# Keys padded with zeros and two heads per product in the scores of a mixer, with some buffers moved

## The chip, the core and the metric

The kernel runs on one core of a Trainium2 chip. The metric is the device time of one whole execution in microseconds (us); smaller is better. A measured time is the median of several runs. A profile is one further execution, recorded by the hardware profiler. The engines are TensorE (PE in the tables; PEld is its weight load), VectorE (DVE), ScalarE (ACT), GpSimd (POOL) and SyncE (SP), which issues most transfers.

## What is computed

The reference is two transformer blocks on 256 tokens of width 1024 in fp32. The change lies in the second block's mixer, which stands twice in the program (stages m0 and m1, two layers):

```python
z = h @ w_in[l]
(na_q, na_k, na_v, gq, gk, gv, gr, gfl, gbl, c_q, c_kv, k_rope, gates) = split_cols_2(z, IN_SPLITS)
qa = rms_norm_2(na_q.reshape(B, S, NA_HEADS, NA_HEAD_DIM), na_q_norm[l])
ka = rms_norm_2(na_k.reshape(B, S, NA_HEADS, NA_HEAD_DIM), na_k_norm[l])
y_na = neighborhood_attention(qa, ka, va, na_rpb[l])
o_gla = gla_bidirectional(gq..., gk..., gv..., g_f..., g_b...)
y_gla = rms_norm_2(o_gla, gla_out_norm[l]).reshape(B, S, GLA_V_W) * silu(gr)
y_mla = mla_attention(c_q, c_kv, k_rope, cq_norm, ckv_norm, w_uq, w_ukv, q_norm, k_norm, cos, sin)
gt = sigmoid(gates.reshape(B, S, N_BRANCH, D))
mixed = gt[:, :, 0] * (y_na @ w_br_na) + gt[:, :, 1] * (y_gla @ w_br_gla) + gt[:, :, 2] * (y_mla @ w_br_mla)
x = x + mixed @ w_out[l]
```

So one mixer has three branches over the same input: neighbourhood attention (NA, 8 heads of 64), gated linear attention (GLA, 4 heads of key width 64 and value width 128, both directions), and latent attention (MLA, 4 heads whose scores add a part of width 128 and a rotary part of width 64).

## The kernel before

A tile scheduler orders the instructions. The Python code says what depends on what and which buffer each value takes; the scheduler plays the program through its own clock and writes one list for each engine. A buffer with the same tag as an older one has the older one's room, so its first writer waits for the older one's last reader. A change of buffers or of an instruction's length therefore changes the lists of all engines in the two mixers; nothing ahead of stage m0 differs.

Weights come as fp32 tiles ("raw"). `prep` splits each into a rounded part (ACT, L149) and a rest (DVE, L153), and `mm3` (L188 to L190) makes three short products of each. Results stand in PSUM banks of [128, 512] from three pools: "pj" (three banks: projections), "pa" (three: scores, transposes, attention values) and "pb" (two: GLA).

In `mixer2`, q and k of NA are transposed (L1346) and copied to "naq" and "nak" with the 64 rows of two heads on top of each other (L1347). `na_scores` makes, for each of two query tiles and each of four pairs of heads, two products on 64 of the 128 array rows (L1357); a pair is two heads that lie in the same half of the rows. DVE adds the bias (L1359). `attention` takes the rest: DVE row maximum (L805), ACT exponential (L807), PE transposes (L815), ACT or DVE copies (L820, L822), PE values (L827), and the close (L833, then the transposes L201).

`gla(f)` is called for two halves of heads, f = 0 and 1. Each is a chain over three engines: gate product (PE, L1452, 32 rows), then ACT L1455, DVE L1456, ACT L1457 (exp), DVE L1458, ACT L1459 (with a load of its function table), five DVE steps (L1460 to L1464), ACT L1470 (again with a table load), DVE L1471, ACT L1474 to L1476, DVE and POOL L1477 to L1479, PE transposes (L1482), an ACT copy (L1483), and only then the state products (PE, L1491, 64 rows), the state steps (DVE, L1499), the inner scores (PE, L1508), the values (PE, L1516 and L1520) and the norm (ACT, L1524). The projection "gr" of GLA's output gate goes from its two pj banks through ACT (L1409) into a buffer "gs" of its own.

`uq_proj` and `ukv_proj` make q, k and v of MLA: squares on ACT (L1561, L1580), scaling on DVE, and `put`, which transposes (PE, L1552 and L1553) and copies to "mq" or "mk" (ACT, L1554). `mla_scores` makes for each head one product on 128 rows (L1600) and one on 64 rows (L1601). The branches' results meet in `mix`, two buffers in the room of "naq" and "nak", gated by `gate` (ACT, L1540).

Of the kernel before, what the change touches and what calls it, by code (L numbers as in the profile page):

```python
# [10 lines left out]
AF = mybir.ActivationFunctionType  # L11
# [55 lines left out]
class Kern:  # L67
# [1223 lines left out]
    def mixer2(self, i, finish):  # L1291
# [31 lines left out]
        nc.gpsimd.memset(hv(rst)[:, :, 0:1], 0.0)  # L1323


        naT = [T([128, 4, 256], "naq"), T([128, 4, 256], "nak")]
        nav = T([128, 2, 512], "nav")
        yna = self.quad()
        na_heads = [[0, 2], [1, 3], [4, 6], [5, 7]]

        def na_proj(j):
            if j == 2:
                self.proj_nat(hT, 8, W, (i,), [(1024, 512)], lambda t, p: nc.scalar.activation(nav[:, t, :], p, AF.Copy))
                return

            def ev_na(t, p):
                sq = g2()
                nc.scalar.activation(sq, p, AF.Square)
                ss = self.small([128, 8], "nss")
                nc.vector.tensor_reduce(ss, hv(sq), axis=AX.X, op=OP.add)  # L1340
                r = self.rstd(ss, 8, 1.0 / 64, "na")
                x = g2()
                nc.vector.tensor_tensor(hv(x), hv(p), r.unsqueeze(2).to_broadcast([128, 8, 64]), op=OP.mult)
                q = self.pa()
                for k in range(4):
                    nc.tensor.transpose(q[:, k * 128:k * 128 + 128], x[:, k * 128:k * 128 + 128], ident)  # L1346
                nc.scalar.activation(naT[j][:, :, t * 128:t * 128 + 128], hv(q, 128), AF.Copy, scale=nag[:, j:j + 1])  # L1347
            self.proj_nat(hT, 8, W, (i,), [(j * 512, 512)], ev_na, first=j == 0)

        def na_scores(t, hs):  # L1350
            bias = T([128, 512], "sE", bufs=2).rearrange("p (h n) -> p h n", h=2)
            s = na_heads.index(hs)
            nc.sync.dma_start(bias, A["na_bias"][i][t][:, 2 * s:2 * s + 2, :])
            q = self.pa()
            b = slice(hs[0] % 2 * 64, hs[0] % 2 * 64 + 64)
            for j, h in enumerate(hs):
                nc.tensor.matmul(q[:, j * 256:j * 256 + 256], naT[0][b, h // 2, t * 128:t * 128 + 128], naT[1][b, h // 2, :],  # L1357
                                 start=True, stop=True)
# [43 lines left out]
            nc.vector.tensor_copy(gk[:, f, :], p[:, :256])  # L1402

        gv = T([128, 2, 512], "gv")
        gs = T([128, 2, 512], "gs")

        def ev_gr(t, p):
            y = gs[:, t, :]
# [36 lines left out]
        def gla(f):  # L1445
# [56 lines left out]
            for b in range(2):  # L1502
                bs = slice(b * 64, b * 64 + 64)
                h = f * 2 + b
                q = self.pb()
                for j in range(4):
                    js = slice(j * 128, j * 128 + 128)
                    nc.tensor.matmul(q[:, js], d_[bs, js], c_[bs, js], start=True, stop=True)  # L1508
                Ah = At[:, b * 256:b * 256 + 256].rearrange("p (t n) -> p t n", t=2)
                qv = q.rearrange("p (d t n) -> p d t n", d=2, t=2)  # L1510
                for d, m in ((0, mF), (1, mB)):
                    nc.vector.copy_predicated(Ah, col(m).to_broadcast([128, 2, 128]), qv[:, d])
                o = self.pb()
                for t in range(2):
                    os = slice(t * 128, t * 128 + 128)
                    nc.tensor.matmul(o[:, os], Ah[:, t, :], gv[:, t, h * 128:h * 128 + 128], start=True, stop=False)  # L1516
                    todo = [(n, d) for n in (2 * t, 2 * t + 1) for d in range(2) if (n > 0 if d == 0 else n < 3)]
                    for n, d in todo:
                        s = n - 1 if d == 0 else 2 - n
                        nc.tensor.matmul(o[n % 2 * 64:n % 2 * 64 + 64, os], c_[bs, d * 256 + n * 64:d * 256 + n * 64 + 64],  # L1520
                                         st[bs, d, s, :], start=False, stop=(n, 1 - d) not in todo or d == 1)
                for t in range(2):
                    jk = T([128, 128], "jk2", BF16)
                    nc.scalar.activation(jk[:, :128], o[:, t * 128:t * 128 + 128], AF.Square, accum_out=gss[:, t, h:h + 1])  # L1524
                    r = self.rstd(gss[:, t, h:h + 1], 1, 4.0 / 128, "g", 4 * EPS)
                    y = gs[:, t, h * 128:h * 128 + 128]
                    nc.vector.scalar_tensor_tensor(y, o[:, t * 128:t * 128 + 128], r, y, op0=OP.mult, op1=OP.mult)
            if f == 1:
                for t in range(2):
                    self.to_T(gs[:, t, :], t, ygl, bank=self.pb)  # L1530


        th = {}
# [7 lines left out]
            self.proj_nat(hT, 8, W, (i,), [(3680 + b * 1024 + n * 512, 512)], ev_g)  # L1541


        mq, mk = T([128, 2, 3, 256], "mq"), T([128, 2, 3, 256], "mk")
        mv = T([128, 2, 512], "mv")
        mss = T([128, 2, 2, 4], "mss")

        def put(t, half, nope, rp, dst):

            q = self.pa()  # L1550
            for k in range(2):
                nc.tensor.transpose(q[:, k * 128:k * 128 + 128], nope(k), ident)  # L1552
            nc.tensor.transpose(q[:, 256:384], rp, ident)  # L1553
            nc.scalar.activation(dst[:, half, :, t * 128:t * 128 + 128], hv(q[:, :384], 128), AF.Copy)  # L1554

        def uq_proj(half):
            def ev_uq(t, p):
                jk = T([128, 192], "jk3", BF16)
                for j in range(2):
                    h = half * 2 + j  # L1560
                    nc.scalar.activation(jk[:, :192], p[:, j * 192:j * 192 + 192], AF.Square, accum_out=mss[:, t, 0, h:h + 1])  # L1561
                r = self.rstd(mss[:, t, 0, half * 2:half * 2 + 2], 2, 1.0 / 192, "uq")
                x = g2()
# [6 lines left out]
                put(t, half, lambda k: x[:, k * 192:k * 192 + 128], o.rearrange("p h n -> p (h n)"), mq)  # L1570
            self.proj_nat([cq], 2, "mla_w_uq_2", (i,), [(half * 384, 384)], ev_uq)

        def ukv_proj(half):
            def ev_kv(t, p):
                pv = hv(p, 256)
                nc.vector.tensor_copy(hv(mv[:, t, half * 256:half * 256 + 256], 128), pv[:, :, 128:256])
# [12 lines left out]
                put(t, half, lambda k: x[:, k * 128:k * 128 + 128], x[:, 256:384], mk)  # L1589
# [4 lines left out]
        def mla_scores(t, hs):  # L1594
            q = self.pa()
            ts = slice(t * 128, t * 128 + 128)
            for j, h in enumerate(hs):
                out = q[:, j * 256:j * 256 + 256]
                b = slice(h % 2 * 64, h % 2 * 64 + 64)
                nc.tensor.matmul(out, mq[:, h // 2, h % 2, ts], mk[:, h // 2, h % 2, :], start=True, stop=False)  # L1600
                nc.tensor.matmul(out, mq[b, h // 2, 2, ts], mk[b, h // 2, 2, :], start=False, stop=True)  # L1601
            return hv(q, 256), T([128, 512], "sE", bufs=2).rearrange("p (h n) -> p h n", h=2)

        def mla_att():
            self.attention(T, [(t, hs) for t in range(2) for hs in ([0, 2], [1, 3])], mla_scores,
                           lambda b, h: mv[:, b, h * 128:h * 128 + 128], 128, ymla, self.pa, self.pa, 1, 0)


        mix = [T([128, 1024], n) for n in ("naq", "nak")]
        xq = [None, None]  # L1610
        done = {}

# [134 lines left out]
def constants(inputs):  # L1747
# [27 lines left out]
    rpb = np.asarray(inputs["na_rpb_2"])[:, [0, 2, 1, 3, 4, 6, 5, 7]]  # L1775
# [30 lines left out]
```

## Time and profile before

| | us |
|---|---|
| median of 3 runs | 2415.28 (2411.58 to 2416.04) |
| time of the profiled execution | 2414.7 |
| span of its trace | 2412.9 |
| PE busy | 2384.6 (99% of the span) |
| DVE, ACT, POOL busy | 1470.6 (61%), 1209.5 (50%), 178.1 (7%) |
| mean granted PE clock | 0.997 |

In the trace m0 lies at about 1290 to 1530 us and m1 at about 1950 to 2190 us. The page's part 1 gives the busy time of each engine; part 4 follows back the chain of work that ended last and gives each engine's share of it. In the rows further below, a timeline row has its start, its duration, the engine, the line, the operation, what it writes and reads, its shape (rows x columns of the stationary operand, then partitions x elements of the moving one) and a count. Matmuls overlap, so a product's cost is the step from its start to the next one's start, not its duration.

### The profile page before, as it was taken

The numbers are of one execution on the slowest core, as the hardware profiler recorded it, in microseconds if no ns is written. First come the engines' busy times: TensorE is split into PE (matmuls) and PEld (weight loads), VectorE is DVE, ScalarE is ACT, GpSimd is POOL, SyncE is SP. The second block draws the span as 40 slices with busy tenths as digits, with TensorE's granted clock in tenths as the row PEclk, the third lists the DMA queues.
The fourth block names the chain that finished last, engine by engine and source line by source line (L and its number), as shares of the span: only waits on it lengthen the run. The fifth ranks groups of instructions, "written<-read, shape, count | busy, mean of one in ns | idle before, by whom it ended". The sixth has DMA issues, their size and how long they took to land.

```text
span 2412.9 us, 31370 instructions
## 1 busy us (share of the span) xinstructions
PE 2384.6 (99%) x11520; PEld 1960.4 (81%) x11520; DVE 1470.6 (61%) x2082; ACT 1209.5 (50%) x1868; POOL 178.1 (7%) x185
## 2 busy tenths in 40 slices
PE   8999999999999999999999999999999999999999
PEld 6888988888888778888888777888888887778887
DVE  6556786555655765556556775655565567756554
ACT  5445554444544545445445563454454455635443
POOL 0000330000000400000001120100000011201000
PEclk9999999999999999999999999999999999999999
DMA  7666535665665426656666533566566574435654
GB/s 246 190 189 182 148 123 177 200 190 170 207 212 168 130 69 203 190 167 209 187 188 189 159 119 111 174 206 190 170 205 191 175 205 143 118 120 168 201 189 134
DMA packets 301258, 417.13 MB, mean 173 GB/s; under 512 B 29168, under 2 KB 227248, under 8 KB 301104
## 3 DMA queue, kind: packets, MB, share of 16 engines
q1 hardware_dynamic: 300960, 414.66, 55.7%
q8 instruction: 90, 1.47, 0.2%
q14 instruction: 64, 0.52, 0.1%
q10 hardware_dynamic: 144, 0.48, 0.0%
HBM read 414.01 MB, written 1.05 MB: 172 GB/s over the span
## 4 chain that ended last, share of the span: by engine, by line
PE 96%; DVE 1%; POOL 1%; DMA 1%; ACT 1%; issue 1%; SPq 0%; POOLq 0%; DVEq 0%; ACTq 0%
PE pb L189 13%; PE pb L188 13%; PE pb L190 13%; PE pj L188 13%; PE pj L190 13%; PE pj L189 13%; PE pa L201 3%; PE pa L188 2%; PE pa L189 2%; PE pa L190 2%; PE pj L59 2%; PE pa L59 1%; PE pa L827 1%; PE pa L1357 1%; PE pa L815 0%
## 5 line engine op out<-in xcount | busy, mean ns | idle before, releaser
L153 DVE TENSOR_TENSOR wl<-raw,wh 128x1024 fp32r<-128x1024 f32 x711 | 879.0, 1242 | 548.1 <-ACT wh L149 544.0
L149 ACT ACTIVATE wh<-raw 128x1024 fp32r<-128x1024 f32 x717 | 753.1, 1055 | 572.2 <-PE pb L190 321.3
L188 PE MATMUL pb<-wh,qh 128*128 128x512 f32 x1408 | 551.3, 392 | 0.8 <-ACT wh L149 0.8
L189 PE MATMUL pb<-wl,qh 128*128 128x512 f32 x1408 | 550.3, 391 | 0.5 <-DVE wl L153 0.5
L190 PE MATMUL pb<-wh,ql 128*128 128x512 f32 x1408 | 549.8, 390 | 0.0
L188 PEld LDWEIGHTS pb<-wh,qh 128*128 128x128 f32 x1408 | 264.6, 188 | 56.5 <-ACT wh L149 1.2
L189 PEld LDWEIGHTS pb<-wl,qh 128*128 128x128 f32 x1408 | 264.6, 188 | 56.0 <-DVE wl L153 1.0
L190 PEld LDWEIGHTS pb<-wh,ql 128*128 128x128 f32 x1408 | 264.7, 188 | 55.5
L188 PE MATMUL pj<-wh,qh 128*128 128x512 f32 (+1 forms) x674 | 267.7, 400 | 0.7 <-ACT qh L204 0.7
L189 PE MATMUL pj<-wl,qh 128*128 128x512 f32 (+1 forms) x674 | 264.9, 393 | 1.2 <-DVE wl L153 1.2
L190 PE MATMUL pj<-wh,ql 128*128 128x512 f32 (+1 forms) x674 | 264.0, 395 | 0.0
L190 PE MATMUL pj<-wh,gl 128*128 128x512 f32 x432 | 173.8, 402 | 0.0
L189 PE MATMUL pj<-wl,gh 128*128 128x512 f32 x432 | 168.5, 390 | 0.0
L188 PE MATMUL pj<-wh,gh 128*128 128x512 f32 x432 | 168.3, 391 | 0.0
L446 ACT ACTIVATE sg<-pb,nr 128x256 f32<-128x256 f32 x176 | 83.4, 474 | 151.7 <-PE pb L190 151.6
L188 PEld LDWEIGHTS pj<-wh,qh 128*128 128x128 f32 x674 | 126.9, 189 | 29.5 <-issue 4.3
L190 PEld LDWEIGHTS pj<-wh,ql 128*128 128x128 f32 x674 | 126.9, 188 | 29.3 <-issue 2.7
L189 PEld LDWEIGHTS pj<-wl,qh 128*128 128x128 f32 x674 | 127.2, 189 | 26.8 <-DVE wl L153 2.0
L448 DVE SCALAR_TENSOR_TENSOR g<-pb,nr,sg 128x256 f32<-128x256 f32 x176 | 84.6, 481 | 93.7 <-ACT sg L446 93.7
L204 ACT ACTIVATE gh<-pa 128x256 fp32r<-128x256 f32 x176 | 67.2, 382 | 129.9 <-PE pa L201 129.8
L273 POOL TENSOR_TENSOR nr<-nm,mhalf 128x1 f32<-128x1 f32 x24 | 14.2, 593 | 1444.7 <-DVE nm L271 1444.7
L205 DVE TENSOR_TENSOR gl<-pa,gh 128x256 fp32r<-128x256 f32 x176 | 74.3, 422 | 71.3 <-ACT gh L204 64.0
(538 smaller groups left out, 2993.0 us busy)
## 6 DMA issues: line engine op xcount, KB each, us to landing
raw<-in_ffn_w SPq DMA_DIRECT2D x352, 256.0 KB, 3.1
raw<-in_w_in SPq DMA_DIRECT2D x104, 512.0 KB, 4.0
raw<-in_ffn_w_gate SPq DMA_DIRECT2D x176, 256.0 KB, 2.9
raw<-in_ffn_w_up SPq DMA_DIRECT2D x176, 256.0 KB, 3.1
raw<-in_ffn_w_down SPq DMA_DIRECT2D x88, 512.0 KB, 3.6
raw<-in_ffn_w SPq DMA_DIRECT2D x88, 512.0 KB, 3.5
raw<-in_hy_w_in SPq DMA_DIRECT2D x44, 512.0 KB, 3.7
raw<-in_hy_w_out SPq DMA_DIRECT2D x16, 512.0 KB, 3.3
```

The costliest lines, as they stand in the source:

```text
L59: self.last = fn(*a, **k)
L149: nc.scalar.activation(h[:, :n], r[:, :n], AF.Copy)
L153: eng.tensor_tensor(l[:, :n], r[:, :n], h[:, :n].bitcast(F32), op=OP.subtract)
L188: mm(out, a[0], b[0], start=start, stop=False)
L189: mm(out, a[0], b[1], start=False, stop=False)
L190: return mm(out, a[1], b[0], start=False, stop=stop)
L201: pe = nc.tensor.transpose(p[:, k * 128:(k + 1) * 128], src[:, k * 128:(k + 1) * 128], self.ident)
L204: act = nc.scalar.activation(hv, pv, AF.Copy)
L205: dve = nc.vector.tensor_tensor(lv, pv, hv.bitcast(F32), op=OP.subtract)
L446: nc.scalar.activation(sg, q[t][:, :256], AF.Silu, scale=rs[t])
L448: nc.vector.scalar_tensor_tensor(g, q[t][:, 256:], rs[t], sg, op0=OP.mult, op1=OP.mult)
L827: at["V", k] = nc.tensor.matmul(acc[t][:, h * dv:h * dv + dv], PT[:, j * 2 + b, :], vals(b, h), start=b == 0, stop=b == 1)
```

## The change

The keys get zeros where the other head of a pair has its rows. "nak" grows to [128, 4, 2, 256]: for each pair the first copy holds the upper head's keys and zeros in rows 64 to 127, the second the reverse. POOL writes the zeros; the one ACT copy of the keys becomes two of 64 rows. One product on all 128 rows with 512 columns then gives the scores of both heads, and a pair is now two neighbouring heads. MLA's rotary keys are padded likewise in a new buffer "mr" [128, 2, 2, 256], so that two 64-row products become one of 128 rows and 512 columns, and the one ACT copy of a key tile becomes three (L1568 and twice L1571). "mk" shrinks by a third.

Room for the larger "nak" is found by moving: "gs" loses its own buffer and takes that of "naq" (free after the last NA score), "mr" takes that of "nav" (free after the last NA value), and `mix` lies wholly in that of "nak". A constant's order of heads follows the new pairs.

```diff
-        naT = [T([128, 4, 256], "naq"), T([128, 4, 256], "nak")]
+        naq, nak = T([128, 4, 256], "naq"), T([128, 4, 2, 256], "nak")
+        nc.gpsimd.memset(nak[64:128, :, 0, :], 0.0)
+        nc.gpsimd.memset(nak[0:64, :, 1, :], 0.0)
...
-                nc.scalar.activation(naT[j][:, :, t * 128:t * 128 + 128], hv(q, 128), AF.Copy, scale=nag[:, j:j + 1])
+                for b in range(2):
+                    bs = slice(b * 64, b * 64 + 64)
+                    nc.scalar.activation(nak[bs, :, b, ts], hv(q[bs], 128), AF.Copy, scale=nag[bs, 1:2])
...
-            for j, h in enumerate(hs):
-                nc.tensor.matmul(q[:, j * 256:j * 256 + 256], naT[0][b, h // 2, t * 128:t * 128 + 128], naT[1][b, h // 2, :],
-                                 start=True, stop=True)
+            nc.tensor.matmul(hv(q, 256), naq[:, hs[0] // 2, t * 128:t * 128 + 128], nak[:, hs[0] // 2], start=True, stop=True)
...
-        gs = T([128, 2, 512], "gs")
+        gs = []
...
+            if not gs:
+                gs.append(T([128, 2, 512], "naq"))
...
-            nc.scalar.activation(dst[:, half, :, t * 128:t * 128 + 128], hv(q[:, :384], 128), AF.Copy)
+            nc.scalar.activation(mk[:, half, :, ts], hv(q[:, :256], 128), AF.Copy)
+            for b in range(2):
+                bs = slice(b * 64, b * 64 + 64)
+                nc.scalar.activation(mr[0][bs, half, b, ts], q[bs, 256:384], AF.Copy)
...
+                mr.append(T([128, 2, 2, 256], "nav"))
+                nc.gpsimd.memset(mr[0][64:128, :, 0, :], 0.0)
+                nc.gpsimd.memset(mr[0][0:64, :, 1, :], 0.0)
...
-            for j, h in enumerate(hs):
-                out = q[:, j * 256:j * 256 + 256]
-                b = slice(h % 2 * 64, h % 2 * 64 + 64)
-                nc.tensor.matmul(out, mq[:, h // 2, h % 2, ts], mk[:, h // 2, h % 2, :], start=True, stop=False)
-                nc.tensor.matmul(out, mq[b, h // 2, 2, ts], mk[b, h // 2, 2, :], start=False, stop=True)
+            nc.tensor.matmul(hv(q, 256), mq[:, p, 2, ts], mr[0][:, p], start=True, stop=False)
+            for j in range(2):
+                nc.tensor.matmul(q[:, j * 256:j * 256 + 256], mq[:, p, j, ts], mk[:, p, j, :], start=False, stop=j == 1)
...
-        mix = [T([128, 1024], n) for n in ("naq", "nak")]
+        mix2 = T([128, 2, 1024], "nak")
+        mix = [mix2[:, 0, :], mix2[:, 1, :]]
```

Lines of the changed code are given with their own numbers; what was L1357, L1409, L1452, L1482, L1491, L1508, L1516 and L1520 is L1364, L1417, L1460, L1490, L1499, L1516, L1524 and L1528 there, the chain L1455 to L1479 is L1463 to L1487, and `put` is L1563 to L1571.

The lists move in m0 and m1. Names in them: "gs" or "naq" the output gate of GLA, "pj_", "pa_", "pb_" the PSUM banks, "wh" and "wl" a weight tile's two parts, "w" the GLA chain's buffers, "th" the branch gates.

ACT around the eviction of gr in m0, before:

```order
L1459 ACT_TABLE_LOAD
L1459 ACTIVATE w_2649_12223<-w_2648_12222 128x512
L807 ACT_TABLE_LOAD
L807 ACTIVATE sE_11675,rs_11674<-sE_11675,snm_11681 128x256 x2
L1409 ACTIVATE gs_11224<-pj_12084 128x512
L1470 ACTIVATE dec_12238<-w_2648_12222 128x4 x2
L1475 ACTIVATE w_2648_12222<-w_2648_12222 128x512
```

The same place now, from the copy that ends half 0's transposes on:

```order
L1491 ACTIVATE w_2649_12225<-pb_12251 128x512
L1603 ACTIVATE jk_2638_12183,mss_11234<-pj_12162 128x128 x2
L807 ACTIVATE sE_11694,rs_11672<-sE_11694,snm_11699 128x256 x2
L807 ACTIVATE sE_11714,rs_11672<-sE_11714,snm_11719 128x256 x2
L149 ACTIVATE wh_12498<-raw_12496 128x768
L1603 ACTIVATE jk_2643_12204,mss_11234<-pj_12163 128x128 x2
L1417 ACTIVATE naq_12152<-pj_12078 128x512
L1417 ACTIVATE naq_12152<-pj_12079 128x512
```

The first eviction of gr stood in the middle of half 0's chain; both now stand behind that chain's last step.

PE in half 0 of GLA in m0, before, about the first state products:

```order
L188 MATMUL pj_12474<-wh_12168,qh_11080 128x512
L189 MATMUL pj_12474<-wl_12169,qh_11080 128x512
L1491 MATMUL pb_12256<-gv_11223,w_2649_12223 128x256
L1491 MATMUL pb_12260<-gv_11223,w_2649_12223 128x256
L190 MATMUL pj_12474<-wh_12168,ql_11081 128x512
L188 MATMUL pj_12474<-wh_12478,qh_11080 128x512
L189 MATMUL pj_12474<-wl_12479,qh_11080 128x512
L190 MATMUL pj_12474<-wh_12478,ql_11081 128x512
```

The same stretch now, from its last weight product to the first value products:

```order
L190 MATMUL pj_12163<-wh_12100,ql_11227 128x512
L1499 MATMUL pb_12278<-gv_11225,w_2649_12225 128x256
L827 MATMUL pa_11689<-nav_11217,sPT_11708 128x64 x4
L1516 MATMUL pb_12283<-w_2648_12224,w_2649_12225 128x128 x4
L815 MATMUL pa_11723<-const_81,sE_11714 128x128 x2
L1364 MATMUL pa_11736<-nak_11214,naq_11213 128x512
L815 MATMUL pa_11723<-const_81,sE_11714 128x128 x2
L1524 MATMUL pb_12290<-gv_11225,w_2649_12225 128x128
L1528 MATMUL pb_12290<-st_12257,w_2648_12224 64x128 x3
```

The long projection that lay between the steps of GLA (the gate of branch 0, "pj_12474") has moved behind half 0.

ACT in half 1 of GLA in m1, before:

```order
L1455 ACTIVATE w_3929_17988<-pb_17990,gb_16852 128x256 x2
L1457 ACTIVATE w_3929_17988<-w_3929_17988 128x512
L1554 ACTIVATE mk_16878<-pa_18314 128x3x128
L1554 ACTIVATE mq_16877<-pa_18256 128x3x128
L149 ACTIVATE wh_18425<-raw_18423 128x1024
L1459 ACT_TABLE_LOAD
L1459 ACTIVATE w_3930_17989<-w_3929_17988 128x512
```

The same place now:

```order
L1568 ACTIVATE mk_16881<-pa_17866 128x2x128
L1571 ACTIVATE nav_17808<-pa_17866 64x128 x2
L1463 ACTIVATE w_3929_17992<-pb_17994,gb_16854 128x256 x2
L1548 ACTIVATE th_18201<-pj_18126 128x512
L149 ACTIVATE wh_18269<-raw_18267 128x1024
L1465 ACTIVATE w_3929_17992<-w_3929_17992 128x512
L1578 ACTIVATE jk_3980_18223,mss_16883<-pj_18203 128x192
L149 ACTIVATE wh_18331<-raw_18329 128x1024
L1578 ACTIVATE jk_3980_18223,mss_16883<-pj_18203 128x192
L1467 ACT_TABLE_LOAD
L1467 ACTIVATE w_3930_17993<-w_3929_17992 128x512
```

Half 1's chain now shares the queue with the squares of uq (L1578) and with a branch gate (L1548), which came before or after it.

## Rows read from the trace of the kernel before

**Rows 1.** The page: busy time of PE and its weight load; chain by engine.
```profile
PE 2384.6 (99%) x11520; PEld 1960.4 (81%) x11520; DVE 1470.6 (61%) x2082; ACT 1209.5 (50%) x1868; POOL 178.1 (7%) x185
PE 96%; DVE 1%; POOL 1%; DMA 1%; ACT 1%; issue 1%; SPq 0%; POOLq 0%; DVEq 0%; ACTq 0%
```

**Rows 2.** Waits of PE: waiting line, releaser: us in total, times, longest.
```profile
PE pa L201 <- DVE sE L833: 3.4, 4, 0.9
```

**Rows 3.** Groups by line and shape: busy us, mean ns | idle before.
```profile
L1357 PE MATMUL pa<-nak,naq 64*128 64x256 f32 x64 | 19.5, 422 | 0.0
L1601 PE MATMUL pa<-mk,mq 64*128 64x256 f32 x32 | 11.1, 428 | 0.0
L1600 PE MATMUL pa<-mk,mq 128*128 128x256 f32 x32 | 10.6, 412 | 0.0
```

**Rows 4.** Timeline of PE around one group of NA scores in m0.
```profile
1315.40 0.28 PE L190 MATMUL pj<-qh,wl 128*96 128x256 f32 x1
1315.61 1.13 PE L1357 MATMUL pa<-nak,naq 64*128 64x256 f32 x4
1316.66 0.39 PE L188 MATMUL pj<-qh,wh 128*128 128x256 f32 x1
1316.89 0.28 PE L189 MATMUL pj<-ql,wh 128*128 128x256 f32 x1
1317.01 0.28 PE L190 MATMUL pj<-qh,wl 128*128 128x256 f32 x1
```

**Rows 5.** Timeline of PE in the MLA scores of m0.
```profile
1438.00 0.59 PE L1600 MATMUL pa<-mk,mq 128*128 128x256 f32 x2
1438.52 0.70 PE L1601 MATMUL pa<-mk,mq 64*128 64x256 f32 x2
1439.15 0.70 PE L1600 MATMUL pa<-mk,mq 128*128 128x256 f32 x2
```

**Rows 6.** Timeline of PE in the first block: an fp32 product with 512 columns.
```profile
311.71 1.02 PE L649 MATMUL pa<-hin,bct 128*128 128x512 f32 x2
312.57 0.60 PE L704 MATMUL pb<-v,kw 128*128 128x257 f32 x2
```

**Rows 7.** Timeline of PE: products on different halves of the rows.
```profile
1396.28 0.48 PE L1357 MATMUL pa<-nak,naq 64*128 64x256 f32 x1
1396.29 0.48 PE L1491 MATMUL pb<-gv,w 64*128 64x256 f32 x1
```

**Rows 8.** Windows: us, then PE, PEld, DVE, ACT, POOL busy (count), clock, DMA share, GB/s.
```profile
1379.41:1406.79 27.38, 27.38 (x143) 21.08 (x142) 22.68 (x50) 13.64 (x38) 5.24 (x7) 1.00 0.52 162
1420.25:1448.15 27.90, 27.90 (x125) 20.95 (x124) 21.26 (x34) 19.58 (x36) 5.15 (x7) 1.00 0.44 132
1411.30:1414.70 3.40, 3.05 (x16) 2.83 (x17) 2.21 (x7) 1.73 (x5) 1.06 (x3) 0.50 0.32 120
```

**Rows 9.** Timeline of ACT in half 1 of GLA in m0; in brackets idle before, releaser.
```profile
1421.29 0.85 ACT L1455 ACTIVATE w<-pb,gb 128x256 f32<-128x256 f32 x2
1423.19 0.63 ACT L1457 ACTIVATE w<-w 128x512 f32<-128x512 f32 x1 [1.05 <-DVE w L1456]
1423.73 0.47 ACT L1554 ACTIVATE mk<-pa 128x384 f32<-128x384 f32 x1
...
1425.40 1.06 ACT L149 ACTIVATE wh<-raw 128x1024 fp32r<-128x1024 f32 x1 [0.82 <-PE pj L190]
1426.48 1.28 ACT L1459 ACT_TABLE_LOAD   x1
...
1432.90 1.28 ACT L1470 ACT_TABLE_LOAD   x1 [0.83 <-DVE w L1463]
...
1442.83 0.60 ACT L1483 ACTIVATE w<-pb 128x512 f32<-128x512 f32 x1 [2.58 <-PE pb L1482]
```

**Rows 10.** Groups of ACT from 1404 to 1450 us by shape: the short kinds.
```profile
L1561 ACT ACTIVATE jk<-pj 128x192 bf16<-128x192 f32 x5 | 1.6, 330 | 1.3 <-PE pj L190 1.3
L1470 ACT ACTIVATE dec<-w 128x4 f32<-128x4 f32 x2 | 0.4, 200 | 0.0
```

More of the change, by code (lines that the diff above doesn't have):

```diff
@@ L1323, in mixer2 @@
         nc.gpsimd.memset(hv(rst)[:, :, 0:1], 0.0)
-        naT = [T([128, 4, 256], "naq"), T([128, 4, 256], "nak")]
+        naq, nak = T([128, 4, 256], "naq"), T([128, 4, 2, 256], "nak")
+        nc.gpsimd.memset(nak[64:128, :, 0, :], 0.0)
+        nc.gpsimd.memset(nak[0:64, :, 1, :], 0.0)
         nav = T([128, 2, 512], "nav")
         yna = self.quad()
-        na_heads = [[0, 2], [1, 3], [4, 6], [5, 7]]
+        na_heads = [[0, 1], [2, 3], [4, 5], [6, 7]]
         def na_proj(j):
@@ L1346, in ev_na @@
                     nc.tensor.transpose(q[:, k * 128:k * 128 + 128], x[:, k * 128:k * 128 + 128], ident)
-                nc.scalar.activation(naT[j][:, :, t * 128:t * 128 + 128], hv(q, 128), AF.Copy, scale=nag[:, j:j + 1])
+                ts = slice(t * 128, t * 128 + 128)
+                if j == 0:
+                    nc.scalar.activation(naq[:, :, ts], hv(q, 128), AF.Copy, scale=nag[:, 0:1])
+                    return
+                for b in range(2):
+                    bs = slice(b * 64, b * 64 + 64)
+                    nc.scalar.activation(nak[bs, :, b, ts], hv(q[bs], 128), AF.Copy, scale=nag[bs, 1:2])
             self.proj_nat(hT, 8, W, (i,), [(j * 512, 512)], ev_na, first=j == 0)
@@ L1354, in na_scores @@
             q = self.pa()
-            b = slice(hs[0] % 2 * 64, hs[0] % 2 * 64 + 64)
-            for j, h in enumerate(hs):
-                nc.tensor.matmul(q[:, j * 256:j * 256 + 256], naT[0][b, h // 2, t * 128:t * 128 + 128], naT[1][b, h // 2, :],
-                                 start=True, stop=True)
+            nc.tensor.matmul(hv(q, 256), naq[:, hs[0] // 2, t * 128:t * 128 + 128], nak[:, hs[0] // 2], start=True, stop=True)
             nc.vector.tensor_tensor(bias, hv(q, 256), bias, op=OP.add)
@@ L1404, in mixer2 @@
         gv = T([128, 2, 512], "gv")
-        gs = T([128, 2, 512], "gs")
+        gs = []
         def ev_gr(t, p):
-            y = gs[:, t, :]
+            if not gs:
+                gs.append(T([128, 2, 512], "naq"))
+            y = gs[0][:, t, :]
             nc.scalar.activation(y, p, AF.Tanh, scale=0.5)
@@ L1525, in gla @@
                     r = self.rstd(gss[:, t, h:h + 1], 1, 4.0 / 128, "g", 4 * EPS)
-                    y = gs[:, t, h * 128:h * 128 + 128]
+                    y = gs[0][:, t, h * 128:h * 128 + 128]
                     nc.vector.scalar_tensor_tensor(y, o[:, t * 128:t * 128 + 128], r, y, op0=OP.mult, op1=OP.mult)
@@ L1529, in gla @@
                 for t in range(2):
-                    self.to_T(gs[:, t, :], t, ygl, bank=self.pb)
+                    self.to_T(gs[0][:, t, :], t, ygl, bank=self.pb)
         th = {}
@@ L1541, in gate, with put @@
             self.proj_nat(hT, 8, W, (i,), [(3680 + b * 1024 + n * 512, 512)], ev_g)
-        mq, mk = T([128, 2, 3, 256], "mq"), T([128, 2, 3, 256], "mk")
+        mq, mk = T([128, 2, 3, 256], "mq"), T([128, 2, 2, 256], "mk")
+        mr = []
         mv = T([128, 2, 512], "mv")
         mss = T([128, 2, 2, 4], "mss")
-        def put(t, half, nope, rp, dst):
+        def put(t, half, nope, rp, keys):
             q = self.pa()
+            ts = slice(t * 128, t * 128 + 128)
             for k in range(2):
@@ L1553, in put @@
             nc.tensor.transpose(q[:, 256:384], rp, ident)
-            nc.scalar.activation(dst[:, half, :, t * 128:t * 128 + 128], hv(q[:, :384], 128), AF.Copy)
+            if not keys:
+                nc.scalar.activation(mq[:, half, :, ts], hv(q[:, :384], 128), AF.Copy)
+                return
+            nc.scalar.activation(mk[:, half, :, ts], hv(q[:, :256], 128), AF.Copy)
+            for b in range(2):
+                bs = slice(b * 64, b * 64 + 64)
+                nc.scalar.activation(mr[0][bs, half, b, ts], q[bs, 256:384], AF.Copy)
         def uq_proj(half):
@@ L1569, in ev_uq @@
                 rope(o, xr, t, 2)
-                put(t, half, lambda k: x[:, k * 192:k * 192 + 128], o.rearrange("p h n -> p (h n)"), mq)
+                put(t, half, lambda k: x[:, k * 192:k * 192 + 128], o.rearrange("p h n -> p (h n)"), False)
             self.proj_nat([cq], 2, "mla_w_uq_2", (i,), [(half * 384, 384)], ev_uq)
         def ukv_proj(half):
+            if not mr:
+                mr.append(T([128, 2, 2, 256], "nav"))
+                nc.gpsimd.memset(mr[0][64:128, :, 0, :], 0.0)
+                nc.gpsimd.memset(mr[0][0:64, :, 1, :], 0.0)
             def ev_kv(t, p):
@@ L1588, in ev_kv @@
                     nc.vector.tensor_scalar(x[:, 256 + j * 64:320 + j * 64], kro[:, t, :], r[:, j:j + 1], None, op0=OP.mult)
-                put(t, half, lambda k: x[:, k * 128:k * 128 + 128], x[:, 256:384], mk)
+                put(t, half, lambda k: x[:, k * 128:k * 128 + 128], x[:, 256:384], True)
             self.proj_nat([(cq[0][:, :, 2:4, :], cq[1][:, :, 2:4, :])], 2, "mla_w_ukv_2", (i,), [(half * 512, 512)], ev_kv)
@@ L1596, in mla_scores @@
             ts = slice(t * 128, t * 128 + 128)
-            for j, h in enumerate(hs):
-                out = q[:, j * 256:j * 256 + 256]
-                b = slice(h % 2 * 64, h % 2 * 64 + 64)
-                nc.tensor.matmul(out, mq[:, h // 2, h % 2, ts], mk[:, h // 2, h % 2, :], start=True, stop=False)
-                nc.tensor.matmul(out, mq[b, h // 2, 2, ts], mk[b, h // 2, 2, :], start=False, stop=True)
+            p = hs[0] // 2
+            nc.tensor.matmul(hv(q, 256), mq[:, p, 2, ts], mr[0][:, p], start=True, stop=False)
+            for j in range(2):
+                nc.tensor.matmul(q[:, j * 256:j * 256 + 256], mq[:, p, j, ts], mk[:, p, j, :], start=False, stop=j == 1)
             return hv(q, 256), T([128, 512], "sE", bufs=2).rearrange("p (h n) -> p h n", h=2)
         def mla_att():
-            self.attention(T, [(t, hs) for t in range(2) for hs in ([0, 2], [1, 3])], mla_scores,
+            self.attention(T, [(t, hs) for t in range(2) for hs in ([0, 1], [2, 3])], mla_scores,
                            lambda b, h: mv[:, b, h * 128:h * 128 + 128], 128, ymla, self.pa, self.pa, 1, 0)
-        mix = [T([128, 1024], n) for n in ("naq", "nak")]
+        mix2 = T([128, 2, 1024], "nak")
+        mix = [mix2[:, 0, :], mix2[:, 1, :]]
         xq = [None, None]
@@ L1774, in constants @@
     dc = np.clip(cc[None, :] - cc[:, None] + 15, 0, 30)
-    rpb = np.asarray(inputs["na_rpb_2"])[:, [0, 2, 1, 3, 4, 6, 5, 7]]
+    rpb = np.asarray(inputs["na_rpb_2"])
     c0 = np.clip(cc[:, None] - 8, 0, 48)
```

## Prediction

> **What bounds the kernel now.** I read the page first, then the waits of PE, its timeline in the score products, and last the windows and ACT's timeline in GLA. The page says that PE is busy for 99% of the span and makes 96% of the chain that ended last [rows 1]. So time goes only if PE's own steps get shorter, and comes only if PE waits. In the mixers it hardly waits: the one line there is 3.4 us in four waits at the close of attention, none longer than 0.9 us [rows 2]. DVE and ACT are busy for 61% and 50%, but in places they are nearer to the limit than that: while half 0 of GLA runs, DVE is busy 22.68 of 27.38 us, and in half 1 ACT is busy 19.58 of 27.90 us, while PE is busy all through both [rows 8]. There PE doesn't wait because long projections stand between the steps of GLA.
>
> **What the change takes away.** A product on 64 rows beside products on 128 rows costs more than its columns. In [rows 4] the short products step by 0.12 us (1316.89 to 1317.01). The step into the group is 0.21 (1315.40 to 1315.61), so 0.09 more; the first product behind it takes 0.23, so 0.11 more; and the four passes of the group take 1.05 (1315.61 to 1316.66). The new form is one product of 512 columns on all rows. [rows 6] has two such products' passes in a row: 0.86 us for two passes (311.71 to 312.57), which is what one NA product of two passes will take. So 1.05 - 0.86 = 0.19 inside, 0.20 at the edges: 0.39 a group. There are 16 groups (two layers, two query tiles, four pairs; 64 passes in [rows 3]): 6.2 us.
>
> In MLA each change between 128 and 64 rows costs: two passes take 0.63 us (1438.52 to 1439.15) [rows 5], where half of a 512-column pass would make 0.43. A pair of heads has eight passes, four times 0.63 = 2.5 us. New: two passes of 512 columns, 0.86, and four of 256, 0.86, together 1.72. That is 0.78 a pair, and 8 pairs (32 passes each of L1600 and L1601 [rows 3]) make 6.2 us. The columns streamed don't change; only the switches go. **Saving: 12.4 us.** The rows are close to what will run, so I bound it by 11 and 14.
>
> **What it adds on PE.** In one place of each layer the scheduler had put an NA score on one half of the rows beside a state product on the other half. They start 0.01 us apart and each lasts 0.48 [rows 7], so one of the two is free. A product on 128 rows can't share. That is some 0.25 us in each layer: **+0.5**. The Trainium skill speaks against this change here: its page "TensorE: Matmul & The Clock Gate" (table under "Why this matters for your kernels") says that products with few rows, placed in different row groups, run concurrently, and padding gives that up. The trace agrees in this one place, but in the groups of [rows 4] all four passes lie on the same half, and none overlaps. By that rule the padding gives up these 0.5 us and no more, since neither kernel puts a pair's two heads on different halves; by rows without any overlap it would give up nothing.
>
> **What it adds elsewhere.** ACT gets one more copy for each key tile of NA and two more for each of MLA, all of half the rows or fewer columns than the copy they replace, 0.47 us [rows 9]; POOL gets four fills in each layer (POOL is busy 5 us of 28 [rows 8]). Neither engine is a bound over the whole mixer, so I cost these at nothing except where they stand in front of GLA's chain (below). The fill of "mr" waits on POOL for the last NA value product and holds what is queued behind it there, the powers of the norms (L218); the transfers on SP keep their number.
>
> **What it moves.** This decides. "gs" now takes the room of "naq", so ACT can't evict gr until the last NA score has read "naq". The products of gr fill two of the three "pj" banks, and these stay occupied. Only one bank is left for projections, and the scheduler runs the rest of GLA's half 0 and of NA with little between. In the lists the long gate projection stands behind half 0 (see the change), and meets the projections of uq and ukv together with half 1, whose products are short.
>
> *Half 0, between its transposes and its first values.* Before, this stretch had 27.38 us of PE work [rows 8]. Now I count there 24 transposes and value passes of NA, three NA groups, the twelve state passes, eight inner-score passes and 6 weight products, at the steps above and at those of the same kinds in the trace some 11.0 us in m0. DVE has 33 instructions there instead of 50. At the stretch's mean (22.68/50 = 0.454 us [rows 8]) they take 15.0 us. So PE can wait up to 4.0 us; at the least nothing, since DVE may come in ahead. In m1 24 more weight products stand in it, and the wait is nearer to nothing at its end but the same at its start. I take 1.6 in each layer, below the middle: **+3.2** (0 to 8).
>
> *Half 1, between its gate product and its first state product.* Before: 27.90 us, PE busy for all of it [rows 8]. In that time the chain passed through ACT and DVE with pauses: 1.05 us before L1457, 0.83 before the second table load, 2.58 before the last copy [rows 9]. Now PE has only 12.6 us of work there in m0 and 13.0 in m1, since the gates' long weight products now stand ahead of the gate product or behind the state products. ACT's list for it in m0: four weight roundings (1.06 each, one of them shorter) 4.0, two table loads 2.57, nine steps on 512 columns at 0.60 to 0.63 5.5, and some 22 short ones between 0.20 and 0.47 [rows 9, 10], 6.3; together 18.4. Back to back they overlap by 0.10 (1423.19 + 0.63 is 1423.82, the next starts at 1423.73 [rows 9]), 3.0 for 30, so 15.4. To that come the chain's pauses, in which ACT has nothing ready: 1.05 + 0.83 and, of the last, the transposes alone, some 0.8: 2.7. So 18.1 - 12.6 = 5.5 us that PE waits, say **+5.4**. In m1 the load is 15.7, and six copies of MLA's keys (1.9) stand right in front of the chain's first step: 15.7 + 2.7 + 1.9 - 13.0 = 7.3, say **+7.2**. The bounds: 15.4 - 12.6 = 2.8 in each layer if the chain's pauses are filled; 27.9 - 13.0 = 15 in each if the chain is no quicker than before.
>
> *Behind it.* The first transposes of uq and the state steps come out in a queue that has no slack left. The nearest row is the close of attention, 0.9 us a wait [rows 2]; I take two in each layer: **+3.6** (0 to 8). One of the two closes in each layer that PE waits for now lies in this stretch and falls away: **-1.7**, half of 3.4 [rows 2].
>
> *Clock.* After such a wait before the trace has stretches in which the granted clock is 0.50, the lower of its two levels: 3.40 us from 1411.30 on [rows 8], where the close of attention in m0 waits. Not every such wait has one. A stretch of 3.4 us costs at most 1.7. I take one more in each layer: **+3.4** (0 to 8).
>
> **Sum.** 3.2 + 5.4 + 7.2 + 3.6 - 1.7 + 3.4 + 0.5 - 12.4 = +9.2. The profiled execution took 2414.7, close to the median of 2415.28, so 2423.9: **2424**. The saving is a sure 12 us of shorter steps; the waits are an uncertain 20.
>
> **The rivals.**
> (1) *The waits are hidden.* DVE and ACT take the chain's steps early enough, because both are idle for a third of the mixer, and only the saving is left: 2414.7 - 12.4 + 0.5 = 2403. For it: 99% busy now, with the same chains. Against it: [rows 8] shows DVE at 83% and ACT at 70% in these very stretches, with twice the PE work beside them.
> (2) *Saving and waits cancel.* With the floors, 2 x 2.8 in half 1, nothing in half 0, 3.6 behind it and one fall of the clock in each layer, 5.6 + 3.6 + 3.4 = 12.6 against 12.4 + 1.7 - 0.5 = 13.6: 2413.7, about the time before. It decides if ACT's pauses fill up with the roundings of weights that the scheduler has put there.
> (3) *Half 1 is no quicker than before.* The chain took 21.5 us from L1455 to L1483 (1421.29 to 1442.83 [rows 9]) because ACT and DVE do other work between its steps; if it takes as long again, PE waits up to 15 us in each layer, and the clock falls twice in each: 2414.7 - 12.4 + 30 + 7 - 1.7 + 0.5 = 2438, with the waits of half 0 about 2440.
> (4) *The fill of "mr" holds POOL* until NA's last value, and the powers (L218) of c and of the outer norms behind it come late: two waits of the close's size in each layer, 3.6, on top of the forecast: 2427. It lies within the forecast's range.
>
> **How the numbers follow.** The forecast, with (4), has 0.58, and (3) 0.06; both are slower but for the forecast's lower edge. (2) has 0.22, (1) 0.14. About 0.2% (4.8 us) is what a measurement of this kernel can tell from no change: 2410.4 to 2420.1. The forecast's own range is 2416 to 2438: its lower end is 5.4 + 7.2 less by half and no fall of the clock, its upper end the halves' upper thirds. Its lower edge gives 0.02 to "same". So faster 0.14, same 0.24, slower 0.62. For 8 in 10 the range leaves out most of (1) and the outer part of (3): 2409 to 2439.
>
> **What would show it.** In the profile after: PE's busy time down by about 12 us with its instructions' count nearly the same; L1364 in steps of 0.43 with no 0.2 at its edges; L1621 and L1623 likewise; in PE's waits new rows at L1490, L1499 and L1563 for ACT or DVE, 15 to 25 us together; stretches at clock 0.50 behind them; L1417 behind the last L1364. The prediction is wrong if those waits are under 8 us together (then (1) or (2)), if the group steps stay near 1.05 us (then the padding doesn't take the switch away), or if the time comes from a stage outside m0 and m1, whose lists are unchanged.

## The result, and the profile after

| | median of the runs, us | ratio to before (95% interval) |
|---|---|---|
| before | 2415.66 (2411.58 to 2416.16, 4 runs) | |
| changed | 2430.77 (2425.07 to 2431.28, 4 runs) | 1.0062 (1.0050 to 1.0074) |

The change makes the kernel slower by 15 us (0.6%). The forecast was 2424. The profiled execution of the changed kernel took 2431.15 us; its page begins:

```profile
span 2429.4 us, 31311 instructions
PE 2383.5 (98%) x11472; PEld 1959.6 (81%) x11472; DVE 1468.8 (60%) x2082; ACT 1217.1 (50%) x1888; POOL 183.1 (8%) x193
PE 94%; ACT 2%; DVE 2%; DMA 1%; POOL 1%; issue 1%; SPq 0%; POOLq 0%; DVEq 0%; ACTq 0%
```

Against [rows 1]: 48 passes fewer on PE, 16 for MLA and 32 for NA, and yet PE is busy for nearly the same time (its shorter steps are nearly met by others that got longer, see the table below), and ACT and DVE have 2% of the chain each instead of 1%. The waits of PE in the mixers, us in total, times, longest (the lines not shown lie outside the mixers or are under 0.8 us):

```profile
PE pa L1563 <- DVE g L1583: 5.0, 1, 5.0
PE pb L1490 <- POOL w L1485: 4.2, 2, 2.5
...
PE pa L1563 <- DVE g L1609: 2.3, 2, 1.3
...
PE pa L201 <- DVE sE L833: 1.8, 2, 0.9
PE pb L1499 <- ACT w L1491: 1.5, 2, 0.8
...
PE pj L188 <- ACT th L1548: 1.1, 1, 1.1
PE pa L815 <- ACT sE L807: 1.0, 2, 0.6
...
PE pb L1516 <- DVE st L1507: 0.9, 1, 0.9
...
PE pb L1499 <- DVE st L1505: 0.9, 1, 0.9
```

Where [rows 2] had one line of 3.4 us, there is now a list. It names the places in GLA's two halves and the transposes of uq and ukv behind them.

The saving is there too. By line and shape (busy us, mean ns), where [rows 3] had 41.2 us in its three lines:

```profile
L1364 PE MATMUL pa<-nak,naq 128*128 128x512 f32 x32 | 17.5, 629 | 0.0
L1623 PE MATMUL pa<-mk,mq 128*128 128x256 f32 x32 | 8.5, 382 | 0.0
L1621 PE MATMUL pa<-nav,mq 128*128 128x512 f32 x16 | 8.2, 593 | 0.0
```

These make 34.2 us, 7.0 less. What the edges of a group cost stands in the steps of its neighbours, so these lines show only a part.

The third thing is the clock. Windows of the changed kernel, columns as in [rows 8]:

```profile
1419.60:1433.40 13.80, 13.03 (x38) 8.77 (x38) 8.20 (x29) 4.81 (x20) 4.59 (x9) 0.51 0.36 108
1436.60:1440.20 3.60, 2.98 (x8) 2.35 (x9) 3.23 (x14) 0.00 (x0) 1.37 (x3) 0.53 0.50 146
2088.60:2092.20 3.60, 3.10 (x9) 2.38 (x10) 3.60 (x11) 0.78 (x3) 2.83 (x5) 0.53 0.02 7
2098.80:2105.80 7.00, 6.06 (x16) 4.53 (x16) 4.26 (x13) 1.59 (x5) 3.24 (x6) 0.51 0.38 111
```

With another fall at 1361.6 these are 30.7 us at the lower level in the two mixers. Before had 10.2: the stretch of 3.4 us in [rows 8], and one in m1:

```profile
2022.29:2029.12 6.83, 6.71 (x19) 4.97 (x20) 5.11 (x11) 4.09 (x6) 1.07 (x1) 0.50 0.44 122
```

They begin at waits or soon behind them: the one at 1419.6 after waits of 1.14 us (until 1415.5) and 1.70 us (until 1418.9).

**Where the 15 us come from.** I took every step of PE in the two mixers (start of one pass to the start of the next) and set it against the median step of the same kind (same shapes of it and its neighbours) in the traces of this case. What is over splits into idle time, steps in the stretches at the lower clock, and the rest. From the first transposes of a mixer to the first step that is the same in both kernels again:

| both mixers, us | usual steps | idle | extra at lower clock | rest | sum |
|---|---|---|---|---|---|
| before | 413.5 | 3.5 | 4.6 | 2.2 | 423.8 |
| changed | 402.0 | 20.0 | 11.7 | 5.0 | 438.8 |
| difference | -11.5 | +16.5 | +7.1 | +2.8 | +15.0 |

How these sums split depends on which steps count as one kind: other choices of neighbours give the usual steps a difference of 9 to 15 us, and the lower clock one of up to 9. The idle time and the sums don't depend on it.

Everything outside the mixers takes 1989.1 us before and 1990.6 after (1.2 of that difference lies before m0, where nothing changed).

**The longest wait, read step by step.** Timeline of the changed kernel in half 1 of m1, rows of several engines:

```profile
2083.67 0.40 PE L190 MATMUL pj<-wh,ql 128*128 128x512 f32 x1
2083.85 0.33 ACT L1578 ACTIVATE jk<-pj 128x192 bf16<-128x192 f32 x1
...
2084.28 1.28 ACT L1467 ACT_TABLE_LOAD   x1
...
2085.58 0.63 ACT L1467 ACTIVATE w<-w 128x512 f32<-128x512 f32 x1
...
2086.11 0.31 ACT L1578 ACTIVATE jk<-pj 128x192 bf16<-128x192 f32 x1
...
2087.25 0.70 POOL L218 TENSOR_TENSOR uqr<-uqm,mhalf 128x2 f32<-128x2 f32 x1 [0.73 <-DVE uqm L216]
...
2087.81 0.23 DVE L1605 TENSOR_SCALAR mss<-mss,krs 128x2 f32<-128x2 f32 x1 [0.63 <-ACT jk L1603]
2087.94 0.69 DVE L1469 TENSOR_TENSOR w<-w,w 128x512 f32<-128x512 f32 x1
2088.54 0.74 DVE L1583 SCALAR_TENSOR_TENSOR g<-pj,uqr,qrow 128x192 f32<-128x192 f32 x2
...
2089.10 0.71 PE L1563 MATMUL pa<-const,g 128*128 128x128 f32 x2 [5.04 <-DVE g L1583]
2089.47 0.78 PE L188 MATMUL pj<-wh,qh 128*128 128x512 f32 x1
...
2090.04 0.63 PE L189 MATMUL pj<-wl,qh 128*128 128x512 f32 x1
```

uq has two token tiles here. On ACT the squares of one (2083.85) come out ahead of GLA's table load and its logarithm (L1467), those of the other (2086.11) behind them. The norms go on to POOL, and the first scaling on DVE (L1583) stands behind a step of ukv that waits for ACT (L1605) and a step of GLA's chain (L1469). Meanwhile PE has the next transposes at the head of its queue. The clock is at its lower level from 2088.7 on, still within this wait: the weight products behind it take 0.63 us instead of 0.40.

**The releaser behind it.** The row that tells why the lists look like this is not a wait of PE. ACT's first eviction of gr in m0, before:

```profile
1370.50 0.60 ACT L1409 ACTIVATE gs<-pj 128x512 f32<-128x512 f32 x1 [0.53 <-PE pj L190]
```

ACT of the changed kernel in m0:

```profile
1378.66 0.60 ACT L1491 ACTIVATE w<-pb 128x512 f32<-128x512 f32 x1 [0.74 <-PE pb L1490]
...
1391.69 0.60 ACT L1417 ACTIVATE naq<-pj 128x512 f32<-128x512 f32 x1 [1.72 <-PE pa L1364]
```

The eviction of gr waits for the last NA score (L1364, 1390.63), since it writes into the room of "naq". The last product of gr, counted in the program's order (the 48th weight product behind the transposes of c), ended at 1376.8, so from there on two of the three pj banks lay full for 15 us (13.5 in m1).

### The profile page after: what moved, and what is told of

Same layout as the page of the kernel before. It is cut to its first block, busy times and chain, and to the rows that moved or that the text cites. A ratio compares the mean times of both kernels' runs of the same rounds, so it can differ in the third digit from the quotient of the medians.

```text
span 2429.4 us, 31311 instructions
## 1 busy us (share of the span) xinstructions
PE 2383.5 (98%) x11472; PEld 1959.6 (81%) x11472; DVE 1468.8 (60%) x2082; ACT 1217.1 (50%) x1888; POOL 183.1 (8%) x193
## 4 chain that ended last, share of the span: by engine, by line
PE 94%; ACT 2%; DVE 2%; DMA 1%; POOL 1%; issue 1%; SPq 0%; POOLq 0%; DVEq 0%; ACTq 0%
PE pb L189 13%; PE pb L188 13%; PE pb L190 13%; PE pj L189 12%; PE pj L188 12%; PE pj L190 12%; PE pa L201 3%; PE pa L188 2%; PE pa L189 2%; PE pa L190 2%; PE pj L59 2%; PE pa L59 1%; PE pa L827 1%; PE pa L1364 1%; PE pa L815 0%
```

## The experiments

Theory R says that this hold of the banks takes the long projections out of the stretches of GLA, and makes the waits. Theory P says that the padding itself does it, by its copies on ACT and its fills on POOL.

**gs in a buffer of its own.** "mk" can take the room of "naq" instead, because MLA's keys are written after the last NA score anyway.

```diff
-                gs.append(T([128, 2, 512], "naq"))
+                gs.append(T([128, 2, 512], "gs"))
...
-        mq, mk = T([128, 2, 3, 256], "mq"), T([128, 2, 2, 256], "mk")
+        mq, mk = T([128, 2, 3, 256], "mq"), []
...
             if not mr:
+                mk.append(T([128, 2, 2, 256], "naq"))
                 mr.append(T([128, 2, 2, 256], "nav"))
```

> The changed kernel, but gs keeps a buffer of its own and mk takes the room of naq (free by the time MLA's keys are written). Theory R (gs in the room of naq holds two pj banks until the last NA score, and so takes the projections away from between GLA's steps): the waits of PE in both mixers fall from 20 us to about the 3.4 of before, the stretches at the lower clock go with them, and the saving of the shorter score products is left: 2415.7 - 12 = about 2404 (2400 to 2408). Theory P (the padding's own extra copies on ACT and fills on POOL make the waits): still about 2430. In the lists between a half's gate product and its first state product stand 78 and 98 weight products again (before 77 and 92, changed kernel 54 and 47 to 54).

2399.42 us (2397.76 to 2400.05), ratio to before 0.9939 (0.9928 to 0.9951): 16 us faster than before, 31 faster than the changed kernel, with the same padding, copies and fills. Its page:

```profile
span 2396.1 us, 31306 instructions
...
PE 2367.7 (99%) x11472; PEld 1950.4 (81%) x11472; DVE 1469.2 (61%) x2082; ACT 1215.3 (51%) x1888; POOL 181.2 (8%) x193
```

Waits of PE in the mixers, the two largest:

```profile
PE pa L201 <- DVE sE L833: 1.8, 2, 0.9
...
PE pj L188 <- DVE g L1583: 1.0, 2, 0.5
```

Timeline of ACT, its eviction of gr in m0:

```profile
1368.64 0.60 ACT L1417 ACTIVATE gs<-pj 128x512 f32<-128x512 f32 x1 [0.53 <-PE pj L190]
...
1374.56 0.60 ACT L1417 ACTIVATE gs<-pj 128x512 f32<-128x512 f32 x1
```

gr is evicted in the middle of half 0's chain again, the waits are gone, and no stretch of the mixers is at the lower clock. Theory P falls: its costs are all still there. It is faster than expected because the 4.6 us that the lower clock cost before are gone too (I had left that out). The saving itself is as expected: the usual steps shrank by 13.5 us and the rest grew by 1.6, 12 together.

**gs in the room of naq, and nothing else.** The kernel before with the reuse alone.

```diff
-        gs = T([128, 2, 512], "gs")
+        gs = []
...
+            if not gs:
+                gs.append(T([128, 2, 512], "naq"))
...
-        mix = [T([128, 1024], n) for n in ("naq", "nak")]
+        mix = [T([128, 1024], n) for n in ("gs", "nak")]
```

> The kernel before, with one thing of the change alone: gs takes the room of naq (and mix that of gs and nak). No padding, no new copies or fills. Theory R: waits of PE of 12 to 20 us more than before, most in m1, where the lists have 54, 30 and 54 weight products at the places where the changed kernel has the same numbers; time 2425 to 2437, with no saving to set against it. Theory P: no waits beyond the 3.4 us of before, 2416.

2449.60 us (2446.36 to 2451.14), ratio 1.0147 (1.0134 to 1.0160). Waits of PE in the mixers, the largest:

```profile
PE pa L1554 <- DVE g L1568: 7.1, 2, 5.0
PE pa L1554 <- DVE g L1588: 5.4, 3, 3.7
...
PE pb L1484 <- POOL w L1479: 2.5, 1, 2.5
```

The same lines of uq and of half 1's transposes wait (L1554 and L1484 are L1563 and L1490 of the changed kernel), 22.7 us in all, 19.2 more than before: within what theory R expected of the waits. The time is beyond it by 13 us, since I had left out the clock. This trace has 51 us at the lower level, and they cost 21.7.

**MLA's part alone, and NA's part alone.** MLA alone is the kernel before with "mr", its three copies and the new `mla_scores`. NA alone has the new "nak" and `na_scores`, MLA's unrotated keys in the room of "naq", its rotary keys unpadded in a buffer "mkr", and gs in its own.

Of NA alone, against the changed kernel:

```diff
-                gs.append(T([128, 2, 512], "naq"))
+                gs.append(T([128, 2, 512], "gs"))
...
-                nc.scalar.activation(mr[0][bs, half, b, ts], q[bs, 256:384], AF.Copy)
+            nc.scalar.activation(mk[0][:, half, :, ts], hv(q[:, :256], 128), AF.Copy)
+            nc.scalar.activation(mkr[:, half, ts], q[:, 256:384], AF.Copy)
```

> The kernel before with MLA's part of the change alone (mr padded, in the room of nav, its fills on POOL, three copies a key tile, one rotary product of 512 columns for two heads); NA and gs as before. Theory R: the saving of 8 pairs by 0.78 us, and no new waits: 2415.7 - 6 = 2409.5. Theory P: new waits at the transposes and copies of MLA's keys eat the saving, 2415 to 2420.

2405.66 us (2404.45 to 2410.25), ratio 0.9968 (0.9957 to 0.9979).

> The kernel before with NA's part of the change alone (nak padded, one product of 512 columns for two heads, two copies a key tile); MLA's products as before, its unrotated keys in the room of naq, gs in a buffer of its own. Theory R: 16 groups by 0.39 us less, and some 0.5 us of lost overlap back: 2409.5 to 2410.5, no new waits. Theory P: 2415 to 2420.

2406.06 us (2403.64 to 2406.25), ratio 0.9966 (0.9954 to 0.9977). Neither has waits beyond those of before (3.6 and 3.1 us against 3.5). In usual steps MLA's part saves 6.1 us and NA's 7.5. Both medians came out some 4 us under what I expected, by the clock in part. The NA profile has 3.4 us at the lower clock against 10.2 before; the MLA profile has 10.2, all in m0, and was itself slower than its median. How often the clock falls differs between executions of the same program. Where the mean clock was 0.999 or 1.000, the fastest execution of before took 2410.53 us, of MLA alone 2404.45 and of NA alone 2403.64: 6.1 and 6.9 less, near the saving that was expected.

**One bank held instead of two.** Only the second token tile of gs lies in "naq".

```diff
-            if not gs:
-                gs.append(T([128, 2, 512], "naq"))
-            y = gs[0][:, t, :]
+            y = gs[t] = T([128, 512], ("gs", "naq")[t])
```

> The changed kernel, but only the second token tile of gs lies in the room of naq; the first has a buffer of its own. So one pj bank instead of two is held until the last NA score. By theory R the waits go with the number of banks held: the list has 60, 54, 84 and 78 weight products at the places in GLA (gate product to first state product and transposes to first values, of half 0 and half 1, in m0) where the changed kernel has 54, 6, 47 and 37 and the fast version 78, 66, 98 and 80. That is near the fast version: waits in the mixers under 6 us, 2399 to 2406. If instead any reuse of naq by gs costs its waits whatever is held, 2415 or more.

2411.93 us (2410.21 to 2413.28), ratio 0.9988 (0.9978 to 0.9998). This lies between the two, but 6 us above what I expected: 10.9 us of waits, not under 6. The counts of weight products alone didn't tell it: 3.5 us of the waits lie in half 0, and 4.8 at the transposes of uq and ukv in half 1.

**The rooms of naq and nav exchanged.** gs is evicted later still.

```diff
-                gs.append(T([128, 2, 512], "naq"))
+                gs.append(T([128, 2, 512], "nav"))
...
-                mr.append(T([128, 2, 2, 256], "nav"))
+                mr.append(T([128, 2, 2, 256], "naq"))
```

> The changed kernel with the two rooms swapped: gs in that of nav (free only after the last NA value), mr in that of naq. Two pj banks are held, and longer. In the list half 0 has 54 and 6 weight products as in the changed kernel, half 1 has 75 and 81, about as many as in the kernel before (92 and 80). Theory R by these counts: the waits of half 0 stay (3 to 8 us in the two mixers together, with a fall of the clock or two), those of half 1 go: 2405 to 2418. If the length of the hold alone decides, it is slower than the changed kernel, over 2431.

2416.74 us (2414.95 to 2418.62), ratio 1.0015 (1.0005 to 1.0024). The time is in the range, the reason is not what I wrote. Waits of PE in the mixers, the largest:

```profile
PE pa L1563 <- DVE g L1609: 6.7, 4, 2.2
...
PE pa L1564 <- DVE mqr L1384: 2.4, 2, 1.2
```

The stretch of half 1 in m0, columns as in [rows 8]:

```profile
1413.00:1428.00 15.00, 9.34 (x43) 6.64 (x43) 14.21 (x39) 12.29 (x35) 8.72 (x11) 1.00 0.39 107
```

16.7 us of waits, 11 of them in half 1, which I had expected to be free of them: the transposes of uq and ukv stand close together here, and DVE is busy for 14.21 of 15.00 us. The time is still 14 us under the changed kernel's, in its profile because the clock stayed at its full level all through, in spite of waits as long as 2.2 us. Counted as above, the two banks are held for 26.7 us in m0, against 14.9 in the changed kernel. A longer hold is not slower as such.

**The room kept, gr later.** The changed kernel with all its buffers, and two calls exchanged, so that gr's products come later.

```diff
-        gr_proj()
         ukv_proj(0)
+        gr_proj()
         gla(0)
```

> The changed kernel with all its buffers as they are, gs still in the room of naq, but with two calls exchanged in the code: ukv_proj(0) stands ahead of gr_proj. The products of gr now come late enough that naq is nearly free when they end, so that their two banks are not held. The list has 79, 72, 94 and 72 weight products at the four places in m0 (changed kernel 54, 6, 47, 37; kernel before 77, 72, 92, 80), in m1 60, 88, 99 and 73. If what costs is the hold of the banks, the waits in the mixers fall to under 8 us and the time to 2399 to 2408. If it is the shared room itself, wherever gr stands, the time stays above 2415.

2404.30 us (2403.45 to 2404.90), ratio 0.9960 (0.9947 to 0.9974). ACT's eviction of gr in m0:

```profile
1391.38 1.08 ACT L1417 ACTIVATE naq<-pj 128x512 f32<-128x512 f32 x2 [4.18 <-PE pa L1364]
```

It still waits for the last NA score, at the same time as in the changed kernel. And the two banks are still held, so the reason that I gave didn't come true: in the program's order the last product of gr is now the 60th behind the transposes of c, it ends at 1381.7, and the hold lasts 9.7 us (11.3 in m1), against 14.9 and 13.5 in the changed kernel. What differs is the work that is left for PE meanwhile. The list runs 22 weight products in this time (24 in m1), the changed kernel's 12: here the short ukv projection is done, and the long one of the branch gate comes next and can go through the third bank. GLA's stretches are covered: 7.8 us of waits, none longer than 1.2, and no stretch of the mixers at the lower clock.

So neither the shared room nor two held banks cost 31 us by themselves. This order with the hold is 5 us slower than gs in its own buffer. What costs is the list that the scheduler makes around the hold, where it leaves nothing long to put between GLA's steps. That last link is read from the lists and from these counts; no run changes the list and leaves the hold as it is.

All kernels in one table, us in both mixers as above, from their profiles:

| | usual steps | idle | extra at lower clock | rest | time at lower clock |
|---|---|---|---|---|---|
| before | 413.5 | 3.5 | 4.6 | 2.2 | 10.2 |
| changed | 402.0 | 20.0 | 11.7 | 5.0 | 30.7 |
| gs in its own buffer | 399.9 | 3.4 | 0 | 3.8 | 0 |
| only gs in naq | 411.5 | 22.7 | 21.7 | 2.7 | 51.2 |
| MLA alone | 407.4 | 3.6 | 4.6 | 2.5 | 10.2 |
| NA alone | 406.0 | 3.1 | 1.6 | 3.5 | 3.4 |
| half of gs in naq | 401.5 | 10.9 | 3.3 | 4.9 | 6.8 |
| gs in nav, mr in naq | 401.0 | 16.7 | 0 | 7.1 | 0 |
| gr later | 400.1 | 7.8 | 0 | 5.2 | 0 |

## Why the prediction was right, and where its sizes were off

- *The saving*, 12.4 us: measured 11.5 in the changed kernel (13.5 with gs in its own buffer, where the parts alone give 6.1 and 7.5). Usual steps and rest together, where the choice of kinds matters least, fall by 12.0 us in that version, by 5.8 for MLA and 6.2 for NA; the forecast had 12.4 - 0.5 = 11.9 for this. The sign that PE's busy time falls by about 12 us didn't come in the changed kernel (it fell by 1.1, since steps at the lower clock are longer). With gs in its own buffer, two NA passes and a short product take 0.97 us together (from 1315.53 to 1316.50), as much as two of 0.43 and a plain 0.12; the edges of [rows 4] are gone. An MLA pair takes 1.72 us there (from 1433.24 to 1434.96), as forecast.
- *The cause*: that the reuse of "naq" by gs makes the waits is shown by two runs: own buffer (waits gone) and reuse alone (waits without padding). That it does so by the hold of two banks, as the prediction has it, is only half of it: with gr later and with the rooms exchanged the banks are held too, and the time is 26 and 14 us shorter. It takes the hold and a list that has little else to run. The forecast counted the work left in the lists, so its sum doesn't rest on the hold alone.
- *Half 0*, 1.6 us in each layer: measured 1.5 in m0 (0.89 at L1499, 0.59 at L815) and 1.8 in m1. As expected by size.
- *Half 1 and behind it*, 7.2 + 9.0 = 16.2 us: measured 5.9 in m0 and 8.7 in m1, 14.6. The sum held; its picture was partly wrong. I had GLA's chain as the last thing to come; the longest wait (5.04 us) is for uq's chain, whose small steps stand between GLA's on ACT and DVE, with POOL in between.
- *The close of attention*, -1.7: the waits there fell from 3.4 to 1.8 us.
- *The clock*, +3.4: this is the term that was mis-sized. The extra steps at the lower clock went from 4.6 to 11.7 us, +7.1. I counted one more fall of 3.4 us in each layer; m0 alone has one stretch of 13.8 us. The row that I went by was the shorter of two in the trace before; the other lasts 6.8 us. Whole executions agree: one of the changed kernel had a mean clock of 0.996 and took 2425.07 us, the others 0.993 or 0.994 and 2430 to 2431.
- *What I had at +0.5*: the rest grew by 2.8. The trace before has not one such pair of passes as in [rows 7] in each layer but two (in m0 also at 1396.60), so the lost overlap is some 0.4 us in each, an estimate from two passes of 0.215, half of the 0.43 in [rows 6]. Besides, the first step after a wait is often longer than usual: by 0.06 us at the close, by 0.22 at the first transposes of uq (0.33 instead of 0.11, with the rooms exchanged, at the full clock). I had priced waits by their idle time alone.
- *The rivals*: (1) and (2) didn't happen; (3) went too far for the chain and was right about the clock; (4), the fill of "mr" on POOL, is excluded, since the version with gs in its own buffer has the same fill and no wait for it; in m0 of the changed kernel the fill is done at 1406.0, and the step of POOL that PE waits for (L1485) starts at 1417.35, after waiting for ACT.

By terms: 19.4 - 1.7 of waits were expected and 16.5 came; 12.4 saved and 11.5 came; 3.9 of clock and rest and 9.9 came. So 9.2 expected, 15.0 measured in the mixers.

Left open: which waits bring the clock down. The wait of 0.9 us at the first close of attention came with a fall in m0 of two traces (changed, NA alone) and not in m0 of before; in m1 it came with one in before (2022.3) and not in the changed kernel. Waits of up to 2.2 us had none with the rooms exchanged.

## What to carry to other kernels

When PE is the bound, a buffer that is given to a new owner to save room should be judged by what the new owner holds while it waits, here two of three PSUM banks, and by what the list can still run beside it. An eviction whose releaser belongs to another branch is a place to look at after a change; whether it costs shows in the work that PE has left meanwhile. Padding to full rows was worth its 12 us once the room was taken from a value that is written late ("mk"). Where a stretch of PE loses its cover, add the slower steps after the waits to the waits themselves.

## What the runs showed of the hardware

- A group of 64-row fp32 products between 128-row products took 0.39 us longer than the same scores with zeros on full rows ([rows 4] and 0.97 us at 1315.53 with gs in its own buffer). For 16 groups of NA and 8 pairs of MLA it came to 12 us net.
- Stretches at clock 0.50 cost here 0.38 to 0.49 us for each us in them (11.7 of 30.7, 21.7 of 51.2, 4.6 of 10.2, 3.3 of 6.8), a little less than half; in the four windows shown of the changed kernel PE is busy for 25.2 of 28.0 us, the rest is waiting.
- Exchanging two calls in the source, with equal work and equal buffers, moved the time by 26 us (2430.77 to 2404.30).
